# Around the routing of a two-expert mixture layer: kept products ahead of logits, logit tiles in banks of their own, three row tiles picked ahead of the first expert product

## The chip, the core and the metric

The kernel runs on one core of a Trainium2 chip. Its time is what one execution takes on the device, in microseconds (us). A core has a matrix engine (TensorE, PE in the profile, with its weight loads as PEld), a vector engine (VectorE, DVE), an activation engine (ScalarE, ACT), GpSimd (POOL), and a queue engine (SyncE, SP), which issues nearly all transfers from HBM here. The engines run their own instruction streams in order and wait for each other through semaphores. Matrix products are written to PSUM, from which VectorE and ScalarE read; everything else lies in SBUF.

## What is computed

One block of a network on 256 rows of 1024 features, fp32. Two mixers and a projection make `mixed`; then

```
x = layer_norm(DN_ALPHA * h + mixed, ln1_g, ln1_b)
ffn = hier_moe(x, ...)
x = layer_norm(DN_ALPHA * x + ffn, ln2_g, ln2_b)

def hier_moe(x, w_group, b_group, w_expert, b_expert, w_gate_up, w_down):
    g_logits = xt @ w_group + b_group                 # 4 groups
    grp = argmax(g_logits)
    e_logits = xt @ w_expert + b_expert               # 32 experts, 8 to a group
    e_in_grp = those of the chosen group
    top_v, top_i = top_k(e_in_grp, 2)
    weights = softmax(top_v) * p_grp
    ...
    gate, up = split(xb @ w_gate_up[e], 2)            # 1024 -> 2 x 512
    return (silu(gate) * up) @ w_down[e]              # 512 -> 1024
```

Each row is sent to 2 of 32 experts. The weights of an expert are 1024 x 1024 for gate and up and 512 x 1024 for down, fp32, so that all experts together are about 200 MB, and each byte is used once.

## The kernel before

**Ahead of the routing** TensorE multiplies in three split products (high by high, low by high, high by low), `mm_T` and `mm_N`. The last of them is the projection `w_out`, whose second half of columns goes to the tile `pso[1]`, rows 0 to 127 in `[:, 0, :]` and rows 128 to 255 in `[:, 1, :]` (row tiles 0 and 1). The last three of its eight steps are kept back for row tile 1 (`kept`) and run in two halves of 256 columns; behind each half `residual(1, ...)` adds the residual on VectorE and takes statistics with `bn_stats` (L841, L843).

**Router logits.** `h_T` transposes the un-normalised rows `hx`, four blocks of 128 features at a time, `logits(t, k0, n)` multiplies them with the router's weights (`pg`, L886), 8 steps to a row tile, and `scale_logits` adds the mean's part and scales by the row's 1/sigma (L890, L892). `stats(sums, i)` makes mean and 1/sigma of a row tile with ten small VectorE instructions, most of which need the one before. `route(t)` picks group and experts on VectorE (L895 to L903), counts places with a triangular product on TensorE (`pp`, L906, and L908, which adds row tile 0's counts for row tile 1), and makes `posm`, each row's place with each expert (L909). `norm1` normalises `hx` in place on ScalarE (L914). `keep_warm` puts idle products (`pi`, L271) on TensorE.

**Picks.** `gather` builds, for the four experts of a quad, a one-hot matrix `oh` from `posm` (`rows_of`, L952; one for each row tile), and products `px` (L947) of `hx` with it pick the rows: `pick(b, k, t)` is 128 features (row block k) from row tile t, and both row tiles add up in PSUM. ScalarE (L971, even k) or VectorE (L968, odd k) then scales a picked block into `xg`. `groups` says which blocks share a PSUM bank and stand between two `yield`s; `feed` is this generator for the first quad, advanced by `next(feed)`.

**Experts.** There are eight quads. A quad has eight steps of gate and up (`gu`, `by_expert`, L1191; a step takes block k of `xg` and 2 MB of weights), then `act_T`, then four steps of down (`py`). In the loop over the quads the first quad advances `feed` ahead of steps 0 and 2; every quad makes the picks of the next one at step 4. `late` (L1121) prepares the output accumulators during the first quad.

**What sets the order.** The engines' streams come out of a scheduler that moves instructions, unless `keep_in_program_order` or `issue_after` pin them. The transfers go through SP in the order of `e_get`. The weights' tiles lie in fixed places of SBUF, and a transfer into a place waits until the products that read what was there have run. When the routing starts, the places hold all of the first quad's weights; the first of the second quad's, the second half of tile `E_NEXT` (issued at L171), waits for step 0 of the first quad.

Of the kernel before, what the change touches and what calls it, by code (L numbers as in the profile page):

```python
# [20 lines left out]
P = 128  # L21
S = 256
D = 1024
KD = D // P
# [25 lines left out]
N_WARM = (6, 1, 1, 5, 0, 14, 4)  # L50
# [14 lines left out]
def kernel(ctx: ExitStack, tc: tile.TileContext, x, w_in, b_in, rows_in, relb, w_proj_a, w_proj_b,  # L65
# [310 lines left out]

    def mm_N(ps, t, k, nk, ah, al, hi, lo, skip=False):
        tsl = slice(t * P, (t + 1) * P)
        for n, (a, b) in enumerate(((ah, hi), (al, hi), (ah, lo))):
            nc.tensor.matmul(ps, a[k][:, tsl], b, start=(k == 0 and n == 0), stop=(k == nk - 1 and n == 2),  # L380
                             skip_group_check=skip)
# [467 lines left out]
    def stats(sums, i):  # L849
# [7 lines left out]
        for _ in range(3):  # L857
            nc.vector.scalar_tensor_tensor(w, y, hv, y, op0=ALU.mult, op1=ALU.mult)
            nc.vector.scalar_tensor_tensor(y, w, 1.5, y, op0=ALU.add, op1=ALU.mult)
        last_stat[:] = [nc.vector.scalar_tensor_tensor(nm, mu, -1.0, y, op0=ALU.mult, op1=ALU.mult)]  # L860
# [15 lines left out]
    def h_T(t, k0, n):  # L876
        pt = big1("pt")
        for k in range(k0, k0 + n):
            nc.tensor.transpose(pt[:, (k - k0) * P:(k - k0 + 1) * P], hx[:, t, k * P:(k + 1) * P], ident)
        nc.scalar.activation(hTr[:, t, k0 % 4:k0 % 4 + n].rearrange("p a b -> p (a b)"), pt[:, 0:n * P], AF.Copy)  # L880

    def logits(t, k0, n):
        if not pg:
            pg.append(big2("pg"))
        for k in range(k0, k0 + n):
            nc.tensor.matmul(pg[0][:, t, 0:40], hTr[:, t, k % 4, :], wge[:, k, :], start=(k == 0),  # L886
                             stop=(k == KD - 1))

    def scale_logits(t, mu, rstd, nm):
        tc.keep_in_program_order(nc.vector.scalar_tensor_tensor(lg[:, t], csum, mu, pg[0][:, t, 0:40], op0=ALU.mult,  # L890
                                                                op1=ALU.add))
        nc.vector.scalar_tensor_tensor(lg[:, t], lg[:, t], rstd, bge, op0=ALU.mult, op1=ALU.add)  # L892

    def route(t):
# [11 lines left out]
        nc.tensor.matmul(pp[:, 0:32], stri, sel[:, t], start=True, stop=(t == 0))  # L906
        if t:
            nc.tensor.matmul(pp[:, 0:32], ones, sel[:, 0], start=False, stop=True)  # L908
# [28 lines left out]
    def gather(pos_of, idx, tl, s=1, groups=(range(0, 4), range(4, 8))):  # L937
# [19 lines left out]
        for b in (0, 1):  # L957
            for k in groups[b]:
                pick(b, k, 0)
        rows_of(1)  # L960
        for b, g in enumerate(groups):
            if b == 1:
                for c in range(2, len(groups)):
                    for k in groups[c]:
                        pick(c, k, 0)
# [43 lines left out]
    stats1(0)  # L1009
# [348 lines left out]
```

## Time and profile before

| | |
|---|---|
| median of 3 runs | 657.25 us (656.7 to 657.37) |
| the profiled execution | 661.88 us |
| its span, first to last instruction | 660.3 us |
| its granted TensorE clock, mean | 0.903 |
| busy share of the span | PE 85%, DVE 35%, ACT 25%, POOL 1% |
| bytes moved | 238.49 MB, mean 361 GB/s |

A time in the rows below is measured from the span's start. The span is the profiled execution without 1.6 us around it, and that execution was 4.6 us longer than the median of the others, so a difference read from the profile is put to the median as a difference.

### The profile page before, as it was taken

To read this page: it belongs to the slowest core of one execution; us is meant where nothing else is said; L and a number is where in the kernel's file an instruction comes from. 1 tells how busy PE (TensorE), PEld (TensorE's weight loads), DVE (VectorE), ACT (ScalarE), POOL (GpSimd) and SP (SyncE) were. 2 spreads that over 40 slices of the span, in tenths; PEclk is the share of its full clock that TensorE was granted. 3 is DMA by queue.
4 is the path that set the end of the run, shared out by engine and by line. 5 is a ranking of instruction groups with operands and counts; after the bars stand their busy time and mean duration, and the time that the engine had idled before them with its cause. 6 is when DMAs were issued, how large, how long until landed. Compare 5 with 4: busy or idle time off the path is not lost.

```text
span 660.3 us, 9603 instructions
## 1 busy us (share of the span) xinstructions
PE 561.7 (85%) x4018; PEld 342.5 (52%) x4019; DVE 229.5 (35%) x531; ACT 162.1 (25%) x321; POOL 9.2 (1%) x32
## 2 busy tenths in 40 slices
PE   8999999999999989987687687758957875989686
PEld 8989898999988463622242152305214221523124
DVE  3698758967578332212012000202200120011017
ACT  4653567965554110000010011001000100101010
POOL 1000000000000000000000000000000000000000
PEclk9999999999999988989599888779887888978679
DMA  8998775676897699999999999999999999999981
GB/s 298 376 361 314 234 255 174 214 274 233 309 376 299 239 424 402 429 428 427 428 426 427 425 429 425 425 429 426 427 429 429 427 427 428 427 429 427 391 237 65
DMA packets 48723, 238.49 MB, mean 361 GB/s; under 512 B 4098, under 2 KB 11939, under 8 KB 37027
## 3 DMA queue, kind: packets, MB, share of 16 engines
q1 hardware_dynamic: 48659, 237.81, 90.4%
q8 instruction: 33, 0.54, 0.3%
q14 instruction: 15, 0.12, 0.1%
q10 hardware_dynamic: 16, 0.01, 0.0%
HBM read 236.75 MB, written 1.06 MB: 360 GB/s over the span
## 4 chain that ended last, share of the span: by engine, by line
PE 65%; DMA 26%; DVE 4%; ACT 3%; issue 1%; SPq 0%; DVEq 0%; ACTq 0%
DMA two<-in_w_gate_up_dram 26%; PE psT L373 18%; PE gu L1191 14%; PE py L1191 10%; PE px L947 8%; PE psN L380 7%; PE pr L1121 1%; PE ph L1098 1%; PE pc L1111 1%; DVE yb L1095 1%; DVE yb L1094 1%; ACT yb L1093 1%; DMA xs<-in_x_dram 1%; ACT hw L1099 1%; PE pl L537 1%
## 5 line engine op out<-in xcount | busy, mean ns | idle before, releaser
L1191 PE MATMUL gu<-two,xg 128*32 128x512 f32 x996 | 169.2, 680 | 63.0 <-DMA two<-in_w_gate_up_dram 58.6
L373 PE MATMUL psT<-two,w_spl 128*128 128x256 f32 x1056 | 134.3, 287 | 0.7 <-ACT w_spl L329 0.6
L373 PEld LDWEIGHTS psT<-two,w_spl 128*128 128x128 f32 x1056 | 129.2, 193 | 4.3 <-ACT w_spl L329 2.0
L1191 PEld LDWEIGHTS gu<-two,xg 128*32 128x32 f32 x996 | 40.6, 121 | 168.4 <-issue 83.9
L330 DVE TENSOR_TENSOR w_spl<-two,w_spl 128x512 fp32r<-128x512 f32 x120 | 82.1, 689 | 45.0 <-ACT w_spl L329 44.3
L329 ACT ACTIVATE w_spl<-two 128x512 fp32r<-128x512 f32 x120 | 75.2, 631 | 72.3 <-PE psT L373 41.4
L968 DVE TENSOR_SCALAR xg<-px,cols 128x128 f32<-128x128 f32 x32 | 12.6, 409 | 188.9 <-ACT xg L971 179.2
L1191 PE MATMUL py<-two,hw 128*32 128x512 f32 x440 | 68.8, 727 | 4.8 <-ACT hw L1099 4.8
L971 ACT ACTIVATE xg<-px,cols 128x128 f32<-128x128 f32 x32 | 13.9, 455 | 227.2 <-PE px L947 222.0
L947 PEld LDWEIGHTS px<-oh,hx 128*128 128x128 f32 x256 | 52.8, 295 | 10.7 <-issue 10.7
L947 PE MATMUL px<-oh,hx 128*128 128x128 f32 x256 | 54.5, 372 | 0.0
L1191 PEld LDWEIGHTS py<-two,hw 128*32 128x32 f32 x440 | 16.6, 130 | 43.7 <-issue 35.1
L1111 PE MATMUL pc<-yb,hw 128*128 128x512 f32 (+2 forms) x72 | 30.4, 561 | 2.0 <-ACT yb L1103 1.5
L1104 DVE COPY yb<-py 128x512 f32<-128x512 f32 x7 | 4.8, 691 | 73.0 <-ACT yb L1103 73.0
L1112 DVE TENSOR_TENSOR acc<-acc,pc 128x512 f32<-128x512 f32 (+2 forms) x36 | 22.5, 626 | 21.9 <-PE pc L1111 21.8
L1094 DVE TENSOR_TENSOR yb<-gu,yb 128x512 f32<-128x512 f32 x8 | 5.5, 691 | 69.9 <-ACT yb L1093 69.9
L380 PE MATMUL psN<-w_spl,two 128*128 128x512 f32 x96 | 23.4, 396 | 0.0
L380 PE MATMUL psN<-w_spl,mix 128*128 128x512 f32 (+1 forms) x105 | 23.2, 376 | 0.1
L1111 PEld LDWEIGHTS pc<-yb,hw 128*128 128x128 f32 x72 | 12.5, 189 | 19.9 <-issue 10.3
L1098 PE MATMUL ph<-ident,yb 128*128 128x128 f32 x32 | 6.3, 324 | 18.1 <-DVE yb L1095 18.1
L380 PEld LDWEIGHTS psN<-w_spl,mix 128*128 128x128 f32 x105 | 18.3, 188 | 3.8 <-DVE hx L841 0.3
L1093 ACT ACTIVATE yb<-gu 128x512 f32<-128x512 f32 x8 | 4.8, 597 | 61.5 <-PE gu L1191 61.5
(223 smaller groups left out, 384.3 us busy)
## 6 DMA issues: line engine op xcount, KB each, us to landing
two<-in_w_gate_up_dram SPq DMA_DIRECT2D x48, 2048.0 KB, 28.1
two<-in_w_down_dram SPq DMA_DIRECT2D x20, 2048.0 KB, 32.1
two<-in_w_gate_up_dram SPq DMA_DIRECT2D x28, 1024.0 KB, 9.8
two<-in_w_in_dram SPq DMA_DIRECT2D x20, 1024.0 KB, 5.9
two<-in_w_down_dram SPq DMA_DIRECT2D x15, 1024.0 KB, 15.0
e_t<-in_w_down_dram SPq DMA_DIRECT2D x5, 1024.0 KB, 12.4
two<-in_w_out_dram SPq DMA_DIRECT2D x4, 1024.0 KB, 5.5
two<-in_w_proj_a_dram SPq DMA_DIRECT2D x2, 1024.0 KB, 5.1
```

Of the source, the lines that this page charges most:

```text
L329: ins = [nc.scalar.activation(hi, w, AF.Copy), nc.vector.tensor_tensor(lo, w, hi.bitcast(F32), op=ALU.subtract)]
L330: nc.vector.tensor_tensor(lo, w, hi.bitcast(F32), op=ALU.subtract)]
L373: nc.tensor.matmul(ps[:, c, :], a[:, c * P:(c + 1) * P], b[k], start=(k == 0 and n == 0 and c % 2 == 0), stop=(k == nk - 1 and n == 2 and ...
L380: nc.tensor.matmul(ps, a[k][:, tsl], b, start=(k == 0 and n == 0), stop=(k == nk - 1 and n == 2), skip_group_check=skip)
L947: nc.tensor.matmul(dst, hx[:, t, part_of(k, s)], oh[:, t, :], start=(k == g[0] and t == 0), stop=(k == g[-1] and t == 1), skip_group_check ...
L968: xg_put[:] = [nc.vector.tensor_scalar(xg[:, k, :], pk, g1_parts[s][:, k:k + 1], b1_parts[s][:, k:k + 1], op0=ALU.mult, op1=ALU.add)]
L971: nc.scalar.activation(xg[:, k, :], pk, AF.Identity, bias=b1_parts[s][:, k:k + 1], scale=g1_parts[s][:, k:k + 1])
L1094: nc.vector.tensor_tensor(sg, gu[:, 0, :], sg, op=ALU.mult)
L1098: nc.tensor.transpose(ph[:, k * P:(k + 1) * P], sg[:, part_of(k, s)], ident)
L1111: nc.tensor.matmul(pc, wT[:, t * P:(t + 1) * P], y_tile()[:, sl], start=True, stop=True)
L1112: nc.vector.tensor_tensor(acc[t][:, sl], acc[t][:, sl], pc, op=ALU.add)
L1191: ins = nc.tensor.matmul(dst[sl], xT[:, sl], ws[e], start=first, stop=last, skip_group_check=True)
```

## The change

Seven edits. (1) From the kept products on, TensorE's products, transposes and logits are held in the order in which they are written, and that order has the second half of the kept products ahead of all of row tile 1's logits. (2) The two row tiles' logits go to PSUM tiles of their own. (3) `stats(1)` is written ahead of `scale_logits(0)`, which is cut in two (`center_logits`, `scale_logits`). (4) The idle products, 5 ahead of `route(0)` and 4 behind it, become 11 ahead of it. (5) In `route(1)` the product with `ones`, which needs row tile 0 alone, goes ahead of the triangular one. (6) The first quad's blocks are grouped 1, 2, 4, 1 in place of 1, 4, 3, `feed` starts behind `route(1)`, and a group's picks of row tile 0 stand next to those of row tile 1, in every quad. (7) The second quad's picks are held behind the first quad's last `xg` on VectorE. The parameters `between` and `ahead` of `stats` are not used by any call.

```
 E_PART = 10
 E_NEXT = 25
 OVER_Q = 4
-N_WARM = (6, 1, 1, 5, 0, 14, 4)
+N_WARM = (6, 1, 1, 11, 0, 14)
 
 W_PL = (0, 1, 2, 3)
 XHI, XLO, XS = 4, 5, 6
...
@@ -374,11 +374,18 @@
                                  start=(k == 0 and n == 0 and c % 2 == 0),
                                  stop=(k == nk - 1 and n == 2 and c % 2 == 1), skip_group_check=True)
 
+    hold = [False]
+
+    def held(ins):
+
+        if hold[0]:
+            tc.keep_in_program_order(ins)
+
     def mm_N(ps, t, k, nk, ah, al, hi, lo, skip=False):
         tsl = slice(t * P, (t + 1) * P)
         for n, (a, b) in enumerate(((ah, hi), (al, hi), (ah, lo))):
-            nc.tensor.matmul(ps, a[k][:, tsl], b, start=(k == 0 and n == 0), stop=(k == nk - 1 and n == 2),
-                             skip_group_check=skip)
+            held(nc.tensor.matmul(ps, a[k][:, tsl], b, start=(k == 0 and n == 0), stop=(k == nk - 1 and n == 2),
+                                  skip_group_check=skip))
 
     def ps_T():
         while len(after) > 1:
@@ -846,7 +853,8 @@
 
     last_stat = []
 
-    def stats(sums, i):
+    def stats(sums, i, between=None, ahead=None):
+
 
         mu, var, hv, y, w, nm = (smv[:, i, c:c + 1] for c in range(6))
         nc.vector.bn_aggr(smv[:, i, 0:2], sums)
@@ -854,9 +862,13 @@
 
         nc.vector.tensor_scalar(y.bitcast(I32), hv.bitcast(I32), -0.5, float(0x5f3759df - 2 ** 30 - 2 ** 22),
                                 op0=ALU.mult, op1=ALU.add)
-        for _ in range(3):
+        for n in range(3):
             nc.vector.scalar_tensor_tensor(w, y, hv, y, op0=ALU.mult, op1=ALU.mult)
+            if n == 2 and between:
+                between(mu)
             nc.vector.scalar_tensor_tensor(y, w, 1.5, y, op0=ALU.add, op1=ALU.mult)
+        if ahead:
+            ahead(y)
         last_stat[:] = [nc.vector.scalar_tensor_tensor(nm, mu, -1.0, y, op0=ALU.mult, op1=ALU.mult)]
         return mu, y, nm
 
@@ -876,19 +888,21 @@
     def h_T(t, k0, n):
         pt = big1("pt")
         for k in range(k0, k0 + n):
-            nc.tensor.transpose(pt[:, (k - k0) * P:(k - k0 + 1) * P], hx[:, t, k * P:(k + 1) * P], ident)
+            held(nc.tensor.transpose(pt[:, (k - k0) * P:(k - k0 + 1) * P], hx[:, t, k * P:(k + 1) * P], ident))
         nc.scalar.activation(hTr[:, t, k0 % 4:k0 % 4 + n].rearrange("p a b -> p (a b)"), pt[:, 0:n * P], AF.Copy)
 
     def logits(t, k0, n):
         if not pg:
-            pg.append(big2("pg"))
+            pg.extend((big2("pg")[:, 0, 0:40], big1("pg")[:, 0:40]))
         for k in range(k0, k0 + n):
-            nc.tensor.matmul(pg[0][:, t, 0:40], hTr[:, t, k % 4, :], wge[:, k, :], start=(k == 0),
-                             stop=(k == KD - 1))
-
-    def scale_logits(t, mu, rstd, nm):
-        tc.keep_in_program_order(nc.vector.scalar_tensor_tensor(lg[:, t], csum, mu, pg[0][:, t, 0:40], op0=ALU.mult,
+            held(nc.tensor.matmul(pg[t], hTr[:, t, k % 4, :], wge[:, k, :], start=(k == 0),
+                                  stop=(k == KD - 1)))
+
+    def center_logits(t, mu):
+        tc.keep_in_program_order(nc.vector.scalar_tensor_tensor(lg[:, t], csum, mu, pg[t], op0=ALU.mult,
                                                                 op1=ALU.add))
+
+    def scale_logits(t, rstd):
         nc.vector.scalar_tensor_tensor(lg[:, t], lg[:, t], rstd, bge, op0=ALU.mult, op1=ALU.add)
 
     def route(t):
@@ -903,9 +917,9 @@
         nc.vector.tensor_tensor(sel[:, t], o12[:, t, 0, :], o12[:, t, 1, :], op=ALU.add)
 
         pp = big1("pp")
-        nc.tensor.matmul(pp[:, 0:32], stri, sel[:, t], start=True, stop=(t == 0))
         if t:
-            nc.tensor.matmul(pp[:, 0:32], ones, sel[:, 0], start=False, stop=True)
+            nc.tensor.matmul(pp[:, 0:32], ones, sel[:, 0], start=True, stop=False)
+        nc.tensor.matmul(pp[:, 0:32], stri, sel[:, t], start=(t == 0), stop=True)
         nc.vector.scalar_tensor_tensor(posm[:, t], pp[:, 0:32], 1.0, sel[:, t], op0=ALU.add, op1=ALU.mult)
 
     def norm1(t):
@@ -954,15 +968,13 @@
 
         rows_of(0)
         yield
-        for b in (0, 1):
-            for k in groups[b]:
-                pick(b, k, 0)
+        for k in groups[0]:
+            pick(0, k, 0)
         rows_of(1)
         for b, g in enumerate(groups):
-            if b == 1:
-                for c in range(2, len(groups)):
-                    for k in groups[c]:
-                        pick(c, k, 0)
+            if b:
+                for k in g:
+                    pick(b, k, 0)
             for k, pk in [(k, pick(b, k, 1)) for k in g]:
                 if k % 2:
                     xg_put[:] = [nc.vector.tensor_scalar(xg[:, k, :], pk, g1_parts[s][:, k:k + 1],
@@ -1007,31 +1019,33 @@
                 e_load()
     residual(0, 512, D, pso[1][:, 0, :])
     stats1(0)
+    hold[0] = True
+    logits(0, 0, 4)
     for c in range(2):
         for k, cur in kept:
             out_mm(1, 1, k, cur, 256 * c, 256 * c + 256)
+        residual(1, 512 + 256 * c, 768 + 256 * c, pso[1][:, 1, 256 * c:256 * c + 256])
         if c == 0:
-            logits(0, 0, 4)
-            logits(1, 0, 4)
             h_T(0, 4, 4)
-        residual(1, 512 + 256 * c, 768 + 256 * c, pso[1][:, 1, 256 * c:256 * c + 256])
+    logits(1, 0, 4)
     e_get(E_SPL)
     assert e_next[0] == E_NEXT and len(splits) == 4 * len(w_srcs)
-    h_T(1, 4, 2)
+    h_T(1, 4, 4)
     logits(0, 4, 4)
-    scale_logits(0, *st1[0])
-    h_T(1, 6, 2)
-    stats1(1)
+    st1[1] = stats(bst[:, 1], 1)
+    center_logits(0, st1[0][0])
+    scale_logits(0, st1[0][1])
     logits(1, 4, 4)
-    scale_logits(1, *st1[1])
+    hold[0] = False
+    center_logits(1, st1[1][0])
+    scale_logits(1, st1[1][1])
     keep_warm(N_WARM[3], ident)
     route(0)
-    keep_warm(N_WARM[6], ident)
     norm1(0)
-    feed = places_of(0, work(0), groups=(range(0, 1), range(1, 5), range(5, 8)))
-    next(feed)
     route(1)
     norm1(1)
+    feed = places_of(0, work(0), groups=(range(0, 1), range(1, 3), range(3, 7), range(7, 8)))
+    next(feed)
     e_get(E_PART)
     next(feed)
 
@@ -1217,7 +1231,7 @@
                 combine(wT_of(q - 1))
                 pending = False
             if k == 4 and q + 1 < NQ:
-                with tc.issue_after(ins):
+                with tc.issue_after(ins), (tc.issue_after(xg_put[0].ins) if q == 0 else nullcontext()):
                     run(places_of(q + 1, work(q + 1)))
                 if q:
                     weigh_quad(q + 1, work(q + 1))
```

The order of SP's transfers is the same in both kernels. How the other engines' streams move at the places that the prediction speaks of:

TensorE behind the last full products of `w_out`, before (`psN` are the kept products, `pt` the transposes, `pg` the logits, `pi` the idle products):

```order
L886 MATMUL pg<-wge,hTr 128x40 x8
L380 MATMUL psN<-w_spl,mix 128x256 x9
L879 MATMUL pt<-ident,hx 128x128 x4
L380 MATMUL psN<-w_spl,mix 128x256 x9
L879 MATMUL pt<-ident,hx 128x128 x2
L886 MATMUL pg<-wge,hTr 128x40 x4
L879 MATMUL pt<-ident,hx 128x128 x2
L886 MATMUL pg<-wge,hTr 128x40 x4
L271 MATMUL pi<-ident 128x128 x5
```

And now:

```order
L898 MATMUL pg<-wge,hTr 128x40 x4
L387 MATMUL psN<-w_spl,mix 128x256 x9
L891 MATMUL pt<-ident,hx 128x128 x4
L387 MATMUL psN<-w_spl,mix 128x256 x9
L898 MATMUL pg<-wge,hTr 128x40 x4
L891 MATMUL pt<-ident,hx 128x128 x4
L898 MATMUL pg<-wge,hTr 128x40 x8
L271 MATMUL pi<-ident 128x128 x11
```

Four of the eight logit products (row tile 1's) that stood ahead of the kept products' first half now stand behind their second half, the transposes of two blocks each are one of four, and row tile 0's last logits follow them.

TensorE from the place counts to the third expert step, before, with the programs' buffer numbers (`px_2572`, `px_2573`, `px_2574` are the banks of block 0, blocks 1 to 4 and blocks 5 to 7; `two0`, `two1`, `two2` the weights of steps 0, 1, 2):

```order
L906 MATMUL pp_2584<-sel_2288,oh0_102 128x32
L908 MATMUL pp_2584<-sel_2288,singles_96 128x32
L947 MATMUL px_2572<-oh0_102,hx_1886 128x128
L947 MATMUL px_2573<-oh0_102,hx_1886 128x128 x4
L947 MATMUL px_2572<-oh0_102,hx_1886 128x128
L947 MATMUL px_2574<-oh0_102,hx_1886 128x128 x3
L947 MATMUL px_2573<-oh0_102,hx_1886 128x128 x4
L1191 MATMUL gu_2606<-two0_619,xg0_2571 32x512 x8
L1191 MATMUL gu_2606<-two1_622,xg0_2571 32x512 x8
L947 MATMUL px_2574<-oh0_102,hx_1886 128x128 x3
L1191 MATMUL gu_2606<-two2_625,xg0_2571 32x512 x8
```

And now (`px_2585`: block 0, `px_2586`: blocks 1 and 2, `px_2587`: 3 to 6, `px_2588`: 7):

```order
L922 MATMUL pp_2567<-sel_2288,oh0_102 128x32
L921 MATMUL pp_2579<-sel_2288,singles_96 128x32
L922 MATMUL pp_2579<-sel_2288,oh0_102 128x32
L961 MATMUL px_2585<-oh0_102,hx_1886 128x128
L961 MATMUL px_2586<-oh0_102,hx_1886 128x128 x2
L961 MATMUL px_2585<-oh0_102,hx_1886 128x128
L961 MATMUL px_2586<-oh0_102,hx_1886 128x128 x2
L1205 MATMUL gu_2603<-two0_619,xg0_2584 32x512 x8
L1205 MATMUL gu_2603<-two1_622,xg0_2584 32x512 x8
L961 MATMUL px_2587<-oh0_102,hx_1886 128x128 x8
L961 MATMUL px_2588<-oh0_102,hx_1886 128x128 x2
L1205 MATMUL gu_2603<-two2_625,xg0_2584 32x512 x8
```

Thirteen picks stood ahead of the first expert step and three between steps 1 and 2; now it is six and ten, and one product in place of two follows row tile 1's choice.

VectorE behind the last `bn_stats` of row tile 1, before (`smv` are the statistics, `lg` the logits in SBUF, here row tile 0's):

```order
L843 BN_STATS bst<-hx 128x6
L890 SCALAR_TENSOR_TENSOR lg<-csum,smv,pg 128x40
L852 BN_AGGR smv<-bst 128x2
L892 SCALAR_TENSOR_TENSOR lg<-lg,smv,bge 128x40
L853 TENSOR_SCALAR smv<-smv 128x1
L895 MAX g_2291<-lg 128x8
L855 TENSOR_SCALAR smv<-smv 128x1
L896 MAX_INDEX gi<-g_2291,lg 128x8
L858 SCALAR_TENSOR_TENSOR smv<-smv 128x1
L897 TENSOR_TENSOR el<-grp_u,gi 128x32
```

And now, where the ten instructions of `stats(1)` stand first; these are its last and the ones behind it, of both row tiles in turn:

```order
L872 SCALAR_TENSOR_TENSOR smv<-smv 128x1
L902 SCALAR_TENSOR_TENSOR lg<-csum,smv,pg 128x40
L906 SCALAR_TENSOR_TENSOR lg<-lg,smv,bge 128x40
L902 SCALAR_TENSOR_TENSOR lg<-csum,smv,pg 128x40
L909 MAX g_2291<-lg 128x8
L906 SCALAR_TENSOR_TENSOR lg<-lg,smv,bge 128x40
L910 MAX_INDEX gi<-g_2291,lg 128x8
L909 MAX g_2291<-lg 128x8
L911 TENSOR_TENSOR el<-grp_u,gi 128x32
L910 MAX_INDEX gi<-g_2291,lg 128x8
L912 SCALAR_TENSOR_TENSOR el<-el,lg 128x32
L911 TENSOR_TENSOR el<-grp_u,gi 128x32
```

Row tile 0's choice used to alternate with row tile 1's statistics, and row tile 1's choice followed alone; now the statistics run alone and the two choices alternate.

## Rows read from the trace of the kernel before

**Rows 1.** Windows: length, each engine's busy us (instructions), granted clock, DMA share, GB/s.

```profile
218.00:220.00 2.00, 2.00 (x21) 1.85 (x24) 0.08 (x1) 0.46 (x1) 0.00 (x0) 1.00 0.03 12
...
254.00:256.00 2.00, 2.00 (x24) 0.54 (x19) 0.00 (x0) 0.00 (x0) 0.00 (x0) 1.00 0.87 303
...
260.00:600.00 340.00, 265.23 (x1465) 107.92 (x1458) 43.95 (x79) 24.71 (x51) 4.78 (x12) 0.86 1.01 427
```

**Rows 2.** Timeline of SP, three issues of weights: start, us, line, what, count.

```profile
221.75 0.33 SPq L171 DMA_DIRECT2D two<-in_w_gate_up_dram  x1
...
239.31 0.38 SPq L213 DMA_DIRECT2D two<-in_w_gate_up_dram  x1
...
254.08 0.33 SPq L213 DMA_DIRECT2D two<-in_w_gate_up_dram  x1
```

**Rows 3.** Us from issue to landing, of issues at 204.25, 239.31 and 254.08.

```profile
two<-in_w_gate_up_dram SPq DMA_DIRECT2D x1, 1024.0 KB, 4.8
...
two<-in_w_gate_up_dram SPq DMA_DIRECT2D x1, 1024.0 KB, 19.7
...
two<-in_w_gate_up_dram SPq DMA_DIRECT2D x1, 1024.0 KB, 7.4
```

**Rows 4.** Timeline of TensorE around the routing: start, us, line, operation, records [idle before].

```profile
204.71 1.87 PE L886 MATMUL pg<-wge,hTr 128*128 128x40 f32 x16
206.41 1.32 PE L380 MATMUL psN<-w_spl,mix 128*128 128x256 f32 x9
...
211.94 1.36 PE L271 MATMUL pi<-ident 128*128 128x128 f32 x10
...
216.29 0.38 PE L906 MATMUL pp<-sel,oh 128*128 128x32 f32 x2 [1.65 <-DVE sel L903]
...
216.73 3.15 PE L947 MATMUL px<-oh,hx 128*128 128x128 f32 x26
219.81 3.64 PE L1191 MATMUL gu<-two,xg 128*32 128x512 f32 x32
223.38 0.94 PE L947 MATMUL px<-oh,hx 128*128 128x128 f32 x6
```

**Rows 5.** Timeline of VectorE around the routing.

```profile
204.91 0.69 DVE L841 SCALAR_TENSOR_TENSOR hx<-hx,psN 128x512 f32<-128x512 f32 x1 [0.68 <-PE psN L380]
...
207.76 0.42 DVE L841 SCALAR_TENSOR_TENSOR hx<-hx,psN 128x256 f32<-128x256 f32 x1 [0.71 <-PE psN L380]
...
210.06 0.43 DVE L843 BATCH_NORM_STATS2 bst<-hx 128x6 f32<-128x256 f32 x1
210.65 0.26 DVE L890 SCALAR_TENSOR_TENSOR lg<-csum,smv,pg 128x40 f32<-128x40 f32 x1 [0.16 <-PE pg L886]
...
212.96 0.19 DVE L903 TENSOR_TENSOR sel<-o 128x32 f32<-128x32 f32 x1
...
214.19 0.16 DVE L895 MAX8 g<-lg 128x8 f32<-128x8 f32 x1
...
215.96 0.19 DVE L903 TENSOR_TENSOR sel<-o 128x32 f32<-128x32 f32 x1
216.94 0.19 DVE L909 SCALAR_TENSOR_TENSOR posm<-pp,sel 128x32 f32<-128x32 f32 x1 [0.79 <-PE pp L908]
217.16 0.49 DVE L952 TENSOR_TENSOR oh<-posm,iota 128x128 f32<-128x128 f32 x2
```

**Rows 6.** Timeline of VectorE at the kernel's end: both row tiles' last statistics, alternating.

```profile
650.54 0.36 DVE L852 BATCH_NORM_AGGREGATE smv<-hw 128x2 f32<-128x48 f32 x1
...
652.55 0.27 DVE L860 SCALAR_TENSOR_TENSOR smv<-smv 128x1 f32<-128x1 f32 x2
```

**Rows 7.** Timeline of ScalarE, the first block of `xg`.

```profile
218.36 0.46 ACT L971 ACTIVATE xg<-px,cols 128x128 f32<-128x128 f32 x1 [3.86 <-PE px L947]
```

**Rows 8.** TensorE between the first quad's two products: timeline, and a window.

```profile
241.05 0.66 PE L1098 MATMUL ph<-ident,yb 128*128 128x128 f32 x4 [2.19 <-DVE yb L1095]
...
241.05:252.63 11.58, 11.58 (x52) 7.82 (x53) 5.90 (x13) 0.98 (x2) 0.00 (x0) 0.56 1.01 419
```

More of the change, by code (lines that the diff above doesn't have):

```diff
@@ L1 @@
 import math
-from contextlib import ExitStack
+from contextlib import ExitStack, nullcontext
 import numpy as np
```

## The prediction

> **What bounds the kernel now.** I read the windows first. From 260 to 600 us the 16 DMA engines are busy at a share of 1.01 and move 427 GB/s [rows 1]: each expert's weights are used once, so behind the routing the kernel takes as long as its bytes do. The one place near the routing where the engines have nothing to move is 218 to 220, with a share of 0.03 [rows 1]. The timeline of SP says why: the places in SBUF are full, and the next load is issued at 221.75 [rows 2], when the first step of the first expert product, which began at 219.81 [rows 4], has read its weights. So what the routing costs is the time up to that issue, and a microsecond taken from it should come off the end, as long as the stream of loads does not run dry again.
>
> There is one place where it nearly does. The first quad's gate and up products free all they can by 239.31, and the next load is issued at 254.08, when the down product has begun [rows 2]. The load issued at 239.31 took 19.7 us to land (at 259.0), the one of 254.08 took 7.4 (at 261.5), and one that found the queue nearly empty, at 204.25, took 4.8 [rows 3]. The load of 254.08 could thus have landed at 258.9: the stall is covered with 2.6 us to spare, and the window 254 to 256 shows how thin that is, with 303 GB/s at a share of 0.87 [rows 1].
>
> **The change, step by step.** All times are the old ones unless I say "now".
>
> *Kept products.* Ahead of them stand 16 records of logits from 204.71 to 206.41, 1.70 us [rows 4]; half of them go behind. That is 0.85, but the kept products write the PSUM tile that the residual at 204.91 still reads for 0.69 us, until 205.60 [rows 5]. I take a start at 205.67, 0.74 earlier. The residual at 207.76 waited for just these products, and the last statistics at 210.06 [rows 5] follow it, so they now start at about 209.34 and end at 209.77. The other end is 0, if something that no row shows holds them.
>
> *Statistics alone.* Then come the ten instructions of `stats(1)`. At the kernel's end two such chains, alternating, take 2.01 us from 650.54 to 652.55 [rows 6]; one alone needs as long, since each instruction waits for the one before it. Row tile 0's logits are centred one step later, now at 211.9 instead of 210.65 [rows 5]: 1.3 us are **lost** here. TensorE is not late for it: it has the same products up to 211.94 [rows 4] and fewer waits.
>
> *Two choices in turn.* From 210.65 to 212.96 [rows 5] VectorE started 21 instructions of two independent chains, 20 steps in 2.31 us, 0.116 each (a `max_index` is two instructions). Alone, row tile 1's choice took 9 steps from 214.19 to 215.96 [rows 5], 0.197 each. Now both choices make 24 instructions in turn: 23 steps of 0.116 are 2.67, and row tile 1's `sel` starts at 214.6, not at 215.96: 1.36 earlier, the loss above included.
>
> The Trainium skill speaks against this step: its page "VectorE: DVE Perf Modes", section "The DRAIN you can't avoid", has the next instruction start only when the pipeline has emptied, so that only the count of instructions matters; the section on two instructions with no wait between them allows an earlier start. By 0.116 against 0.197 the trace agrees with the second; by the first, 23 steps would take 4.5 us, which is the third rival below.
>
> *Idle products.* Eleven in a row are 22 records from about 211.9. Ten records took at most 1.36 [rows 4], so 22 end by 214.9 at the latest and, without the length of a last record in each, near 214.3. Row tile 0's `sel`, two steps ahead of the other's, is done near 214.6. The cost is between 0 and 0.2 on TensorE; I take 0, because row tile 1's counts, not row tile 0's, come last.
>
> *One product behind the choice.* From `sel` at 215.96 to the first count at 216.29 is 0.33; `posm` came 0.65 behind that [rows 4, 5], with two products between. One is now ahead: 0.4 to 0.65, and I take 0.43, less by one product (26 records in 3.08 give 0.24 for a product's pair [rows 4]). The one-hot matrix follows at 0.22 and takes about 0.28 (two in 0.49) [rows 5]. From `sel` to the one-hot matrix's end this is 0.33 + 0.43 + 0.22 + 0.28 = 1.26: row tile 0's is ready near 215.6, and row tile 1's at 215.9, or some 0.2 later where its product queues behind row tile 0's.
>
> *Six picks ahead in place of thirteen.* 26 records from 216.73 to 219.81 [rows 4] are 0.237 us for a pick. With 0.14 for a signal to TensorE (as from the end of `sel` to the count), row tile 0's three picks now start near 215.8 and row tile 1's first near 216.5. ScalarE began `xg` at 218.36, 0.44 behind the start of that pick, the sixth of the run, and took 0.46 [rows 7]. Now that is 217.4, and with 0.14 again the first expert step starts at **217.5** instead of 219.81, 2.3 earlier. Of the seven picks' 1.66 (7 x 0.237) some 0.9 is won here, because `xg` now ends the wait where the picks did.
>
> *The other side of the regrouping.* Those seven picks now stand ahead of step 2, behind the three whose last record ended near 224.3 [rows 4]. Step 2 and all that TensorE does behind it is hence only 2.3 - 1.66 = 0.64 earlier. By then steps 0 and 1 have released 3.5 MB, 8 us of loads at 427 GB/s, so the loads are not short of places here.
>
> *The rest.* Logits in two PSUM tiles take away a wait, and the hold on the second quad's picks adds one on TensorE: behind it stand the picks and step 5. But the ten picks end near 223.5 and five blocks of `xg` in turn, at under 0.5 each, near 226, while step 4, three steps of 1.8 (two took 3.57 [rows 4]) behind the picks, ends near 228.9. SP's order is unchanged, the picks issue no transfer, and nothing new stands in POOL's queue. In the later quads the regrouped picks lie under loads. All of these I put at 0.
>
> **Sum.** The first load behind the routing is issued 2.3 us earlier, now at 219.4. At 254.08 TensorE is 0.64 earlier and the queue 2.3: the 2.6 to spare become 0.94, and the stream still holds. The profiled execution, 661.88, becomes 659.6; on the median of 657.25 it is 654.95, **655.0 us**. A measurement of this kernel can tell about 0.2% (1.3 us) from no change.
>
> **The rivals.**
>
> *TensorE's lead is all that comes through* (656.6). If the stream does run dry at 254.08, the loads follow TensorE, and only its 0.64 is left; in between, part of it. For it: the profile's 303 GB/s there [rows 1]; it takes only 0.94 us of bad luck between 239 and 254. Against it: 4.8 us is enough for a load that finds an empty queue [rows 3].
>
> *Slower: TensorE's clock falls in the routing* (659.1). The granted clock is 1.00 (2.4 GHz) from 218 to 220 [rows 1], though TensorE had stood for 1.65 us up to 216.29 [rows 4]. After a wait of 2.19 up to 241.05 it was 0.56 over 11.58 us [rows 8], mostly the 1.2 GHz level, which costs 11.58 x 0.44 = 5.1 us. The same fall behind the routing would put the issue of 254.08 at 258.5 and its landing at 263.3, 1.8 later than before. It decides from the point where TensorE is 2.6 us later than before at 254. For it: the stretch from 214.6 to 217.5 now holds only counts and six picks. Against it: no single wait in it reaches the 1.65 us that left the clock at 1.00.
>
> *Alternating buys nothing* (656.9). If each step of the two choices takes 0.197, row tile 1's `sel` starts at 216.5 and the first step at 219.4: 0.4 is won. Then the change does not do what its order of VectorE says. For it: nothing in these rows; two different MAX_INDEX instructions in turn were not seen before.
>
> **Chances.** Forecast 0.60 (its own range 654.3 to 655.8); TensorE's lead 0.18; alternating buys nothing, or the first step comes no earlier for another reason, 0.11; slower 0.08; more than forecast, up to the 2.3 + 0.94 = 3.2 us at which TensorE at 254 limits, 0.03. Faster by over 0.2% (below 655.9): 0.63; within 0.2%: 0.29; slower: 0.08. The range for 8 in 10 runs from 654.0, the limit just named, to 657.0, which takes in the second and third case and leaves the slower one out.
>
> **What would show it.** In the new trace: kept products near 205.7; `sel` of row tile 1 near 214.6 and steps of 0.12 between the two choices; the first expert step near 217.5; SP's issue near 219.4; step 2 only 0.6 earlier than the old 224.3; the load behind the long gap issued near 253.4, and no window of 2 us between 240 and 264 far below 400 GB/s but the one at 254. The prediction is wrong if the first expert step comes later than 218.5, if the clock shows 0.5 between 217 and 230, or if the issue behind the gap comes later than 254.4.

## The result, and the profile after

The changed kernel took 654.74 us (median of 20 runs, 652.42 to 659.15) where the kernel before took 658.64 in the same sitting: a ratio of 0.9948, 95% interval 0.9928 to 0.9967. On the 657.25 of the table above that is 653.8, 1.2 below the forecast of 655.0. A second comparison gave 0.9982 (0.9952 to 1.0012), which is 656.1. The first tells the change from none and the second does not; taken as estimates they make the kernel 3.4 and 1.2 us faster.

In the first comparison the runs of the changed kernel fall into a lower group (652.42 to 655.58 us) and an upper one (657.82 to 659.15). The profiles tie this to what TensorE's clock does near 630 us (last section), and a median moves with how many runs lie in which group. The runs of the kernel before part less clearly, near 659; below that gap the medians are 657.73 and 654.21 in the first comparison and 657.09 and 654.61 in the second, 3.5 and 2.5 apart. Two times of the profile, which the clock near 630 cannot touch, stand beside each ratio below. Both are counted from the first logits, because that product began anywhere from 202.99 to 204.71 in 14 profiles of kernels whose TensorE has the same instructions up to there: to the **first expert step**, and to the landing of the **last weights** of gate and up.

TensorE's timeline of the changed kernel around the routing answers to [rows 4]:

```profile
203.97 0.98 PE L898 MATMUL pg<-wge,hTr 128*128 128x40 f32 x8
204.91 1.34 PE L387 MATMUL psN<-w_spl,mix 128*128 128x256 f32 x9
...
211.05 2.70 PE L271 MATMUL pi<-ident 128*128 128x128 f32 x22
213.98 0.38 PE L922 MATMUL pp<-sel,oh 128*128 128x32 f32 x2 [0.23 <-DVE sel L917]
...
215.06 1.58 PE L961 MATMUL px<-oh,hx 128*128 128x128 f32 x12 [0.25 <-DVE posm L923]
216.74 3.64 PE L1205 MATMUL gu<-two,xg 128*32 128x512 f32 x32
220.31 2.50 PE L961 MATMUL px<-oh,hx 128*128 128x128 f32 x20
222.74 1.49 PE L1205 MATMUL gu<-two,xg 128*32 128x512 f32 x12
```

VectorE's timeline of the changed kernel answers to [rows 5]; L902 centres a row tile's logits, L917 is `sel`:

```profile
208.60 0.43 DVE L850 BATCH_NORM_STATS2 bst<-hx 128x6 f32<-128x256 f32 x1
...
211.15 0.25 DVE L902 SCALAR_TENSOR_TENSOR lg<-csum,smv,pg 128x40 f32<-128x40 f32 x1
...
214.04 0.19 DVE L917 TENSOR_TENSOR sel<-o 128x32 f32<-128x32 f32 x1
```

From the first logits at 203.97 to the first expert step at 216.74 are 12.77 us; they were 15.10 [rows 4]. The idle records end as the counts begin (0.23 idle, where TensorE stood for 1.65), six picks stand ahead of the step, and ten behind it, so that step 2 begins at 222.74, only 0.8 earlier behind the first logits (before: near 224.3 [rows 4]). SP's timeline, with the first issue behind the routing, the one behind the long gap, and the last of gate and up:

```profile
218.67 0.33 SPq L171 DMA_DIRECT2D two<-in_w_gate_up_dram  x1
...
252.50 0.33 SPq L213 DMA_DIRECT2D two<-in_w_gate_up_dram  x1
...
585.92 0.38 SPq L189 DMA_DIRECT2D two<-in_w_gate_up_dram  x1
```

The us from issue to landing, of the load issued at 237.79 (the last ahead of the gap), the one at 252.50 and the one at 585.92:

```profile
two<-in_w_gate_up_dram SPq DMA_DIRECT2D x1, 1024.0 KB, 16.5
...
two<-in_w_gate_up_dram SPq DMA_DIRECT2D x1, 1024.0 KB, 4.7
...
two<-in_w_gate_up_dram SPq DMA_DIRECT2D x1, 2048.0 KB, 29.6
```

The first load behind the routing is issued 14.70 behind the first logits, where it was 17.04 [rows 2, 4]. The last weights land at 615.5, 411.6 behind them; before, it was 413.6. Of 2.33 us at the first step, 2.05 are thus left at the end. The windows show that this is no straight line:

```profile
220.67:226.67 6.00, 6.00 (x60) 3.19 (x62) 1.66 (x5) 0.92 (x2) 0.76 (x2) 1.00 1.01 404
250.00:252.00 2.00, 2.00 (x14) 0.69 (x14) 0.50 (x2) 0.38 (x1) 0.00 (x0) 0.51 0.67 279
252.00:254.00 2.00, 2.00 (x24) 0.48 (x16) 0.00 (x0) 0.00 (x0) 0.00 (x0) 1.00 0.37 86
254.00:256.00 2.00, 2.00 (x24) 0.60 (x20) 0.00 (x0) 0.00 (x0) 0.00 (x0) 1.00 0.85 356
```

Read the last two numbers of each row, the DMA share and GB/s. From 2 to 8 us behind their first issue the loads move at 404 GB/s; the same stretch of the kernel before has 327:

```profile
223.75:229.75 6.00, 6.00 (x55) 2.05 (x54) 1.39 (x4) 0.46 (x1) 0.77 (x2) 1.00 0.92 327
```

But from 250 to 256 the engines stand idle for 2 x (0.33 + 0.63 + 0.15) = 2.2 us; before, one window lost 0.26 there [rows 1]. **The stream ran dry at the place that the prediction called nearly dry.** Some 2 us are given back there, and 2.05 are left all the same, so something must have been won ahead of it that the forecast did not have.

### The profile page after: what moved, and what is told of

Same layout as the page of the kernel before. It is cut to its first block, busy times and chain, and to the rows that moved or that the text cites. A ratio compares the mean times of both kernels' runs of the same rounds, so it can differ in the third digit from the quotient of the medians.

```text
span 657.0 us, 9610 instructions
## 1 busy us (share of the span) xinstructions
PE 556.4 (85%) x4022; PEld 337.1 (51%) x4023; DVE 230.2 (35%) x531; ACT 162.9 (25%) x320; POOL 9.2 (1%) x32
## 4 chain that ended last, share of the span: by engine, by line
PE 62%; DMA 27%; DVE 6%; ACT 3%; issue 1%; SPq 0%; DVEq 0%; ACTq 0%
DMA two<-in_w_gate_up_dram 26%; PE psT L373 17%; PE gu L1205 14%; PE py L1205 10%; PE px L961 8%; PE psN L387 6%; DMA xs<-in_x_dram 1%; PE ph L1112 1%; PE pc L1125 1%; PE pr L1135 1%; DVE yb L1108 1%; DVE yb L1109 1%; ACT yb L1107 1%; ACT hw L1113 1%; PE pl L544 1%
## 5 line engine op out<-in xcount | busy, mean ns | idle before, releaser
L1205 PE MATMUL gu<-two,xg 128*32 128x512 f32 x996 | 167.3, 657 | 66.3 <-DMA two<-in_w_gate_up_dram 61.7
L1205 PEld LDWEIGHTS gu<-two,xg 128*32 128x32 f32 x996 | 37.1, 117 | 173.4 <-DMA two<-in_w_gate_up_dram 89.5
L1205 PE MATMUL py<-two,hw 128*32 128x512 f32 x440 | 66.0, 703 | 4.8 <-ACT hw L1113 4.8
```

The lines of the kernel that those rows point to most:

```text
L1205: ins = nc.tensor.matmul(dst[sl], xT[:, sl], ws[e], start=first, stop=last, skip_group_check=True)
```

## The experiments

All ratios are to the kernel before, run on the same chip by turns. Behind each result, in brackets: first expert step and last weights, us behind the first logits (before: 15.10 and 413.6; changed: 12.77 and 411.6).

**The two halves.** First edits 6 and 7 alone (groups, picks), then edits 1 to 5 alone (order of the logits, idle products). The later start of `feed`, which belongs to edit 6, is in the second half. Of the first half's edit this shows the line of the groups:

```
-groups=(range(0, 1), range(1, 5), range(5, 8))
+groups=(range(0, 1), range(1, 3), range(3, 7), range(7, 8))
```

> The kernel before with the regrouped picks alone (and the hold on the second quad's picks). Lead theory: the end follows the first load behind the routing. Six picks ahead of the first expert step in place of thirteen bring that step 1.2 us earlier (not 1.66, since the first xg then ends the wait), and the time falls by 1.2 us. Rival: the stream of loads runs dry at the first quad's down product, where TensorE releases places. There TensorE is 0.5 us later than before (1.66 of picks moved behind, 1.2 won), so the time stays or rises by up to 0.5 us.

> The changed kernel with the old groups of picks, so with the order of products, logits, statistics and choices alone. Both theories: row tile 1's choice 1.3 us earlier, one product less behind it, the first expert step 1.4 to 1.7 us earlier, and everything on TensorE behind it by the same; the time falls by 1.4 to 1.7 us. By the view that alternating instructions buys nothing on VectorE: 0 to 0.4 us.

The regrouping alone: 0.9993, 0.9968 to 1.0017 (14.49; 413.8). The order of the logits alone: 0.9999, 0.9977 to 1.0022 (14.17; 412.6), which misses its forecast of 1.4 to 1.7 us. Neither half shows a gain in its ratio. Both together show one in the first comparison and not in the second, so the ratios do not tell whether the halves add up. By the last weights that depends on which profile of the kernel before is taken: against the first (413.6) the halves make -0.2 and 1.0 and both together 2.05, against the second (414.8, below) 1.0 and 2.2 and both together 3.2.

The regrouped kernel in TensorE's timeline, then SP's first issue behind the gap:

```profile
203.28 1.87 PE L886 MATMUL pg<-wge,hTr 128*128 128x40 f32 x16
...
215.24 2.60 PE L947 MATMUL px<-oh,hx 128*128 128x128 f32 x12
...
254.10 0.33 SPq L213 DMA_DIRECT2D two<-in_w_gate_up_dram  x1
```

Its windows (the first begins 2 us behind its first issue):

```profile
222.30:228.30 6.00, 6.00 (x59) 3.19 (x62) 1.66 (x5) 0.91 (x2) 0.76 (x2) 1.00 1.03 417
252.00:254.00 2.00, 2.00 (x18) 0.70 (x18) 0.51 (x2) 0.38 (x1) 0.00 (x0) 0.72 0.43 176
254.00:256.00 2.00, 2.00 (x24) 0.51 (x20) 0.00 (x0) 0.00 (x0) 0.00 (x0) 1.00 0.42 82
```

The regrouping fills the queue early and fast (417 GB/s), and the last load ahead of the gap lands 51.6 behind the first logits, where it was 54.3. The release behind the gap does not move with it: it comes at 50.8, between 49.4 and 50.9 in the two profiles of the kernel before. The first of the two had TensorE's clock up in the routing; the second did not, nor did the regrouped kernel, whose 12 records of picks take 2.60 us (1.58 in the changed kernel). So the stream stands for 2.3 us at 252 to 256. With the order of the logits alone, at a clock that stayed up, the release and the queue move forward by 0.9 and 1.1 from the first profile, nothing runs dry, and the last weights land 1.0 earlier. Together, the second half brings forward a part of the release that the first needs.

**Is the dry stretch real?** `late`, which prepares the accumulators, and the first two weighings stand between the first quad's two products, and TensorE runs them mostly at half its clock [rows 8]. Behind the down product they are out of the way of the release.

```
-        if q == 0:
-            late()
-            weigh_quad(0, tl)
-            weigh_quad(1, work(1))
         py = big2("py")
...
+            if q == 0:
+                with tc.issue_after(ins):
+                    late()
+                    weigh_quad(0, tl)
+                    weigh_quad(1, work(1))
```

> The changed kernel with the preparation of the accumulators (late, and the first two weigh_quad) behind the first quad's down product, which releases the next places some 6 to 9 us sooner. Lead theory (the routing alone sets the end): same time, within 0.3 us. Rival (the stream runs dry there): the window with a DMA share near 0.5 some 35 us behind the routing is gone and the time falls by about 2 us (0.48 of 4 us).

> The kernel before with the same move. Both theories: nearly nothing, since the stream there had 2.6 us to spare; at most the 0.26 us of the window at share 0.87.

In the changed kernel 0.9948, 0.9926 to 0.997 (12.77; 409.9); in the kernel before 1.0007, 0.9982 to 1.0032 (16.72; 414.4). The move brings the last weights 1.7 us forward in the changed kernel, and 0.4 in the one before (from 414.8, its profile with the same fall of the clock in the routing), whose stream had no dry stretch to lose: as expected of the stall, though the first ratio is no better than the changed kernel's own. So both ran once more side by side.

> The changed kernel once more, on one chip with the version whose preparation of the accumulators is moved. First step 12.8 us behind the first logits at a clock of 1.00, the stream dry near 250 to 254; 0.993 to 0.997 of before.

> The changed kernel with the preparation of the accumulators and the first two weighings behind the first quad's down product, beside the changed kernel on one chip. If the dry stretch of the stream sets the changed kernel's time: 1.4 to 2.2 us below it (its last weights landed 2.2 us earlier). If something later gives that back: the same within 0.6 us, as the first comparison of each with before had it.

The changed kernel: 0.9982, 0.9952 to 1.0012, median 656.65 (12.77; 411.6). With the move: 0.9927, 0.9896 to 0.9958, median 653.39 (12.77; 409.2). The first misses its forecast (0.993 to 0.997). Windows of the one without the move (the granted clock is the number ahead of the DMA share):

```profile
250.00:256.00 6.00, 6.00 (x58) 1.79 (x54) 0.50 (x2) 0.38 (x1) 0.00 (x0) 1.00 0.62 228
624.00:638.00 14.00, 11.13 (x94) 4.64 (x95) 4.18 (x12) 2.10 (x4) 0.00 (x0) 1.00 1.02 296
```

The same windows of the one with the move:

```profile
250.00:256.00 6.00, 6.00 (x51) 3.56 (x53) 6.00 (x16) 0.77 (x2) 0.00 (x0) 1.00 1.03 427
624.00:638.00 14.00, 12.23 (x64) 3.87 (x68) 1.78 (x4) 1.19 (x2) 0.00 (x0) 0.76 0.80 235
```

From 250 to 256 the engines are busy throughout with the move, and for 0.62 of the time without. Six of 12 runs without it lie in the upper group, and 2 of 9 with it; within the lower group the medians are 654.6 and 653.4. That is what I can stand for: 1.2 us there (1.4 to 2.2 were forecast), 1.7 to 2.5 by the last weights, and the lowest ratio of the study.

Then ten idle products were put ahead of TensorE's third step: in the changed kernel, in the one with the move, and in the kernel before.

```
             elif q == 0 and k == 2:
                 with tc.issue_after(ins):
                     run(feed)
+                keep_warm(10, ident)
```

> The changed kernel with ten idle products, about 2.45 us of TensorE (11 of them were 2.70 us), between the first quad's second and third expert steps. My theory: in the changed kernel the stream of loads runs dry near 252 us and goes on only when the first down product frees places, so TensorE's time there comes through in full: about 2.4 us above the changed kernel, near 0.9985 of before, with the long gap of SP ending near 255 and a window 250 to 256 that moves less than half of 427 GB/s. The rival, that the stream there does not set the time and the changed kernel gains elsewhere: within 0.6 us of the changed kernel, near 0.995.

> The same ten idle products in the changed kernel whose preparation of the accumulators and first two weighings are moved behind the first quad's down product. There SP's gap ended at 243.9 and loads were queued until 254.1, so TensorE has some 8 us to spare. My theory: the 2.45 us cost nothing, the time is that of this kernel without them (0.9948 of before). The rival, that TensorE's lateness costs wherever it stands: about 2.4 us more, 0.9985.

> The kernel before with the same ten idle products between its second and third expert steps. By landings it had 2.6 us to spare at the release of 254.08, but the two profiles that ran dry lost 1.3 to 1.9 us more than landings tell. My theory: 1 to 2.4 us slower than before (1.0015 to 1.0037). If landings tell the spare time rightly: no slower. Of the first loads behind the routing: in the three kernels with the old groups some 30 of the 8 KB packets took over 450 ns, in the three with the new groups under ten. If the pause of TensorE between steps 1 and 2 makes them quick, this kernel shows under ten as well; if it is another part of the new grouping, some 30 as before.

Changed: 1.0022, 0.9991 to 1.0052 (12.76; 412.3). With the move: 0.9943, 0.9917 to 0.9969 (12.76; 409.8). Before: 1.003, 0.9995 to 1.0065 (16.63; 416.4). TensorE 2.4 us later costs nothing that shows where the queue is long (0.9943 beside 0.9948 and 0.9927; last weights at 409.8 beside 409.9 and 409.2). Where the stream runs dry the ratio loses the whole gain, but the last weights only 0.8 us. The idle products in the timeline of the changed kernel with them:

```profile
222.48 2.40 PE L271 MATMUL pi<-ident 128*128 128x128 f32 x20
```

Its windows:

```profile
240.00:244.00 4.00, 2.38 (x20) 2.22 (x21) 1.99 (x4) 0.71 (x2) 0.00 (x0) 1.00 0.98 406
250.00:252.00 2.00, 2.00 (x14) 0.26 (x10) 0.27 (x3) 0.26 (x1) 0.00 (x0) 0.64 0.74 303
252.00:254.00 2.00, 2.00 (x21) 0.62 (x24) 0.44 (x2) 0.38 (x1) 0.00 (x0) 1.00 0.15 49
```

It is dry as forecast (49 GB/s in the last row), but its last weights are only 0.8 later, not 2.4: in this execution the clock was still 1.00 up to 244 and then at half for 7 us, against some 10 in the changed kernel's. The rise of the median, 4.9 us by the two ratios where 2.4 were forecast, is more than the delay: 8 of its 12 runs lie in the upper group, against 7 of 20. In the lower group its median is 656.3, that of the kernel with the move and the idle products 653.1 (below 655). No profile of it lies in the upper group (660.7 to 663.5), so what those runs lose is not shown. The kernel before with idle products, first the window from 2 us behind its first issue:

```profile
223.76:229.76 6.00, 6.00 (x57) 3.67 (x60) 1.38 (x4) 0.46 (x1) 0.71 (x2) 1.00 0.90 330
254.00:256.00 2.00, 2.00 (x18) 0.49 (x14) 0.57 (x3) 0.51 (x2) 0.00 (x0) 0.98 0.60 242
256.00:258.00 2.00, 2.00 (x24) 0.65 (x20) 0.00 (x0) 0.00 (x0) 0.00 (x0) 1.00 0.53 119
```

It too runs dry now, and loses 1.9 us in these two windows and the next; the ratio agrees with a loss of 1 to 2.4 us, but its interval reaches to nothing. And 25 of its 8 KB packets took over 450 ns, at 330 GB/s: the pause between steps 1 and 2 is not what makes the early loads quick.

**The clock in the routing.** In the regrouped kernel, and in two of the kernel before with other edits, TensorE's clock had fallen at 214 to 220, which the one profile of the prediction did not show.

```
-N_WARM = (6, 1, 1, 11, 0, 14)
+N_WARM = (6, 1, 1, 5, 0, 14)
```

> The changed kernel with 5 idle products ahead of row tile 0's choice in place of 11. By my working TensorE waits there anyway and the products cost or give nothing: the time of the changed kernel (0.9948 of before), clock 1.00 through 214 to 222. The rival, that the run of idle products holds TensorE's clock up in the routing (in two profiles of kernels with 5 and 4 it was down to 0.5 to 0.6 there): a granted clock below 0.8 in a window of 214 to 222, the first expert step 1 to 2 us later, and 0.9965 to 0.998 of before.

> The kernel before with 11 idle products in place of 5 ahead of row tile 0's choice (the 4 behind it stay): the fourth edit by itself. The clock theory: TensorE's clock usually falls in the routing with few idle products (profiles of 4 of 6 kernels with 4, 5 or 9 of them) and not with 11 (0 of 4), which makes the first expert step 1.2 to 1.5 us later; here the granted clock is 1.00 through 214 to 222, the first step starts 15.1 us behind the first logits and not 16.6, and the time is 0.5 to 1.5 us shorter (0.9977 to 0.9992). The prediction's own term: the idle products cost and give nothing, 1.0000, and a clock that falls here too.

> The kernel before, unchanged, profiled once more, since the prediction rests on one profiled execution of it. By the clock theory that one was the rarer case: here the granted clock is below 0.8 in a window of 214 to 222 and the first expert step starts about 16.6 us behind the first logits. By the prediction's reading it is 1.00 and 15.1.

(The count in the second of these is off: up to then the clock had fallen in 4 of 5 profiles with few idle products and in none of 5 with 11.) The changed kernel with 5: 0.9958, 0.9938 to 0.9979 (13.92; 412.9), where the rival had 0.9965 to 0.998. The kernel before with 11: 0.9987, 0.9959 to 1.0015 (15.01; 412.8). The kernel before once more: (16.73; 414.8). Its timeline of TensorE, and SP's first issue behind the gap:

```profile
203.93 1.87 PE L886 MATMUL pg<-wge,hTr 128*128 128x40 f32 x16
...
215.51 0.38 PE L906 MATMUL pp<-sel,oh 128*128 128x32 f32 x2 [1.65 <-DVE sel L903]
...
215.95 4.78 PE L947 MATMUL px<-oh,hx 128*128 128x128 f32 x26
220.66 1.92 PE L1191 MATMUL gu<-two,xg 128*32 128x512 f32 x16
...
254.86 0.33 SPq L213 DMA_DIRECT2D two<-in_w_gate_up_dram  x1
```

Its windows, with the granted clock:

```profile
214.00:216.00 2.00, 0.49 (x5) 0.52 (x5) 1.20 (x7) 0.00 (x0) 0.00 (x0) 1.00 0.98 367
216.00:218.00 2.00, 2.00 (x14) 2.00 (x14) 0.69 (x3) 0.00 (x0) 0.00 (x0) 0.66 0.41 166
218.00:220.00 2.00, 2.00 (x12) 2.00 (x11) 0.00 (x0) 0.46 (x1) 0.00 (x0) 0.50 0.00 0
```

TensorE stands for 1.65 us up to 215.51, as long as in [rows 4]; but here the clock falls to the lower level, and the 26 records of picks take 4.78 us where they took 3.15 [rows 4]. In the same kernel with 11 idle products they take 3.15 again (timeline of TensorE):

```profile
203.44 1.87 PE L886 MATMUL pg<-wge,hTr 128*128 128x40 f32 x16
...
215.38 3.15 PE L947 MATMUL px<-oh,hx 128*128 128x128 f32 x26
218.45 1.92 PE L1191 MATMUL gu<-two,xg 128*32 128x512 f32 x16
```

at a clock of 1.00 (windows):

```profile
214.00:216.00 2.00, 1.55 (x14) 1.39 (x13) 1.15 (x8) 0.00 (x0) 0.00 (x0) 1.00 0.88 330
216.00:218.00 2.00, 2.00 (x20) 2.00 (x19) 0.30 (x2) 0.46 (x1) 0.00 (x0) 1.00 0.25 100
```

And the changed kernel with 5 shows the fall, with 12 records of picks in 2.90 us instead of 1.58 (timeline of TensorE):

```profile
202.99 0.98 PE L898 MATMUL pg<-wge,hTr 128*128 128x40 f32 x8
...
213.00 0.38 PE L922 MATMUL pp<-sel,oh 128*128 128x32 f32 x2 [1.57 <-DVE sel L917]
...
214.08 2.90 PE L961 MATMUL px<-oh,hx 128*128 128x128 f32 x12 [0.23 <-DVE posm L923]
216.91 1.55 PE L1205 MATMUL gu<-two,xg 128*32 128x512 f32 x12
```

and in its windows the clock is at half from 214 to 216:

```profile
214.00:216.00 2.00, 1.92 (x9) 1.95 (x10) 0.37 (x2) 0.00 (x0) 0.00 (x0) 0.50 0.79 293
```

Over the whole study the clock fell here in 5 of 6 profiles of kernels with few idle products and in none of 8 with 11 ahead of the choices. With 11, TensorE's wait for row tile 1's `sel` was 0.23 to 0.45 us, with few 1.57 to 1.65. The fall and its cure are shown in the profile, at a cost of 1.15 to 1.7 us at the first step. What that is worth in time is within the intervals of these ratios and was not told from nothing by them.

## Why the forecast came out, and where it was wrong

**The chain up to the first expert step was right.** Behind the first logits (204.71 in the prediction's numbers):

| | forecast | measured |
|---|---|---|
| kept products start | 0.96 | 0.94 |
| last statistics of row tile 1 | 4.63 | 4.63 |
| row tile 0's logits centred | 7.19 | 7.18 |
| `sel` of row tile 1 | 9.89 | 10.07 |
| first expert step | 12.79 | 12.77 |
| first load issued | 14.69 | 14.70 |
| load behind the long gap issued | 48.69 | 48.53 |

Within the chain two small misses cancel: `sel` comes 0.18 later than forecast, and the way from it to the first step is 0.20 shorter.

"Alternating buys nothing" fell: the 24 instructions of the two choices start from 211.15 to 214.04, 0.126 us each, forecast 0.116. By the 0.197 of a lone chain they would have taken 4.5. The Trainium skill, page "VectorE: DVE Perf Modes", section "The DRAIN you can't avoid", has the next instruction wait until the pipeline is empty, and names as its exception an instruction that is not held. The trace of these two independent chains agrees with the exception.

**The step that failed is the slack:** "At 254.08 TensorE is 0.64 earlier and the queue 2.3: the 2.6 to spare become 0.94, and the stream still holds." TensorE was 0.84 earlier, but the queue 4.0: the last load ahead of the gap landed 50.3 behind the first logits and not 52.0, since the first loads behind the routing moved faster. From 2 to 8 us behind the first issue, the six profiles with the old groups show 272 to 364 GB/s, the eight with the new ones 387 to 419. The stream ran dry, so the windows from 250 to 254 are far below the 400 GB/s that the prediction asked of them.

That was the first rival, but its price was wrong. By the prediction's own numbers a stream that follows TensorE there gains 0.64 + 2.6 = 3.2 us, the limit that it names under "more than forecast", and not 0.64. The dry stretch gave back 2 us, not all of the lead.

The 2.6 rested on one profile. By the same working the second profile of the kernel before had 0.8: its clock had fallen, and its last load ahead of the gap landed 35.4 behind the first issue, where the first profile took 37.2 and the changed kernel 35.6. So how much of the faster queue is the change's own is not settled.

Landings also mis-size such spare time. It was worked out as the queue's last landing, 2.5 for the next load's length, less the release and 4.8. By this the changed kernel was short by 0.5, the regrouped by 1.6, the changed one with ten idle products more by 0.9, and the kernel before with those had 0.4 left; their windows lost 2.2, 2.3, 2.4 and 1.9 us, so the loss hardly follows the shortfall. With 0.8 or more left (the kernel before, in both profiles, and with 11 idle products ahead) no more than 0.3 was lost. By these the forecast's 0.94, had it been left, might have held; but the streams that ran dry lost 0.7 to 2.3 us more than landings tell. The Trainium skill, page "DMA: Bandwidth & Descriptors", section "Why a DMA increments its semaphore by 16 and not by 1", says that a transfer runs on up to 16 engines that finish independently and is complete with the last. The windows agree: 0.33 of the engines' time was idle at 250 to 252, while the load that landed at 254.27 was still under way.

**The term put at nothing was not nothing:** "The cost is between 0 and 0.2 on TensorE; I take 0". With eleven the clock stayed up in the routing in all 8 profiles. Of the 6 profiles with few, the prediction's was the only one in which it stayed up; against the other profile of the kernel before, the first step is won not by 2.3 but by 4.0 us, and the last weights by 3.2. The rival "slower" had the fall on the wrong side: it was in the kernel before.

Against the profile that it was worked out from, the terms are thus 2.3 at the first step, 1.7 more at the queue, and 2.0 lost at the dry stretch (2.2, where the kernel before lost 0.26): 2.0 in all, and the last weights came 2.05 earlier. Against the second profile, 1.6 more are won at the clock. The forecast of 2.3 us lies between the two comparisons, 3.4 and 1.2, with its main term exact and errors that offset each other; that the number came out so near is in part luck. More than half of the gap between the comparisons is the mix of the two groups, since within the lower group they give 3.5 and 2.5; the rest stays open.

## What to carry to other kernels

When a stream of loads has two places that can hold it up, a gain at the first is worth no more than the spare time at the second and what the change wins there; look for that spare time in the engines' idle share, not in landings alone, and clear the second place in the same change, as the moved `late` did. Profile the kernel before more than once when the argument needs a clock that stayed up beside an idle wait, or a spare time of 2 or 3 us: here the clock fell in 5 of 6 profiles and not in the one at hand, and the spare time was 2.6 in one profile and 0.8 in the next. Where two halves of a change each measure as nothing, compare what each does to times in the profile before dropping either.

## What had not been expected of the hardware

**Two groups of runs.** At the last quad's down product the clock either stays at 1.00 or falls. Windows of two kernels from 624 to 638 stand above, with 1.00 and 0.76; the 32 records of that product take 3.64 us in TensorE's timeline of the changed kernel (run beside the move), where the clock stayed:

```profile
627.52 3.64 PE L1205 MATMUL py<-two,hw 128*32 128x512 f32 x32 [0.69 <-ACT hw L1113]
```

and 6.51 in that of the kernel with the move, where it fell:

```profile
626.57 6.51 PE L1205 MATMUL py<-two,hw 128*32 128x512 f32 x32 [0.69 <-ACT hw L1113]
```

that is 2.9 us more at the end of the kernel. From the last weights' landing to the end are 37.7 to 38.2 us in eight profiles with the clock up there, 41.1 to 42.0 in six with it down. Both occur in the same kernel (before: 42.0 and 38.1). What decides between them was not tried.

**Slow packets behind an idle queue.** With the old groups 18 to 32 of the 8 KB packets of the first 14 us took over 450 ns, with the new ones 3 to 17; their median is 309. The pause of TensorE is not the cause (above); what is, stays open.
